# Turning three tiles by 32-column blocks by way of DRAM, with a clock for SyncE's queue in the planner

## The chip, the cores and the metric

The kernel runs on one core of one Trainium2 chip. The metric is the device time in microseconds of one execution. A profiled execution gives, beside its time, a trace of the instructions of each engine: PE (TensorE), DVE (VectorE), ACT (ScalarE), POOL (GpSimd) and SP (SyncE, which here only issues DMAs).

## The reference

One layer of a sequence mixer over 512 frames of 2048 channels. A combined projection feeds two groups of heads, RWKV-7 (16 heads of 64) and HGRN2 (8 heads of 128). Their gated outputs pass one output projection and a layer norm.

```python
proj = jnp.einsum('btd,dc->btc', h, w_in[l])
rw = _token_shift(proj[..., :RWKV_COLS], shift_mu[l])
hg = proj[..., RWKV_COLS:]
o_rwkv, v_first = _rwkv7_branch(rw, ...)
o_hgrn = _hgrn2_branch(hg, ...)
y = jnp.einsum('btc,cd->btd', jnp.concatenate([o_rwkv, o_hgrn], axis=-1), w_out[l])
h = _layer_norm(ALPHA * h + y, ln_w[l], ln_b[l])
...
# RWKV-7, per head, frame by frame, with a = -kk and b = kk * ah:
sa = jnp.einsum('bhij,bhj->bhi', S, a_t)
S = S * w_t[:, :, None, :] + sa[..., None] * b_t[:, :, None, :] + v_t[..., None] * k_t[:, :, None, :]
o_t = jnp.einsum('bhij,bhj->bhi', S, r_t)
```

## The kernel before

**The main stream.** The projections are made of tiles of 128 output channels by 512 frames, 16 steps of 128 input channels each. An fp32 product is made of three float32r matmuls (high by high, high by low, low by high), issued by `three` (line 453). Weights come in loads of 128x1024 into one of two buffers wr (`load`, line 430). Each half is split into a high part wh by ACT and a low part wl by DVE; there are three buffers of each, and `ready` asks for a part two parts ahead of its use. This stream of main matmuls is written out in order.

**The planner.** Everything else runs as Python generators that yield operations. A `Plan` keeps an estimated clock for each engine. After each main matmul it pumps its queues: it starts an operation on DVE, ACT or POOL when the operands are estimated to be ready, and it puts a small matmul between the main ones when its operands are due at least 0.35 us earlier (`LEAD`). What is decided is the order of each engine's instructions; on the chip semaphores hold an instruction until its operands are there. A DMA is issued on SP as the planner comes to it, and `plan.ready` gets an estimated landing time.

**The RWKV pairs.** Two heads make a pair, eight pairs in all, and two pairs make a group. `rwkv_prep` makes, per pair, tiles of 128 channels by 8 chunks of 64 frames: ar (from kk and r) and bk (beta and k). After the scores are made from them, bk is turned, so that the frames of a chunk stand on the partitions: `turned` (line 392) transposes the 32x32 blocks with DVE into a tile tmp and then moves each of the 4 x 4 blocks to its place with a DMA of its own (line 401), SBUF to SBUF, back into bk. The same is done with v into partitions 64 to 127 of a tile z ("zz"), with 4 x 2 blocks. Behind each four (or two) DMAs the generator waits for 0.4 us of PE's clock per DMA. Between the two turns stands the product that sums r k r_k over a head: ACT and DVE split r (tiles "ksq"), two matmuls with a block of ones follow, and the result times v is S["bv"].

**The scan.** `rwkv_group` inverts the scores of a group, adds what v alone gives (`from_v`, which writes partitions 0 to 63 of z), and then `rwkv_scan` goes through the 8 chunks: a product of the state with ar, one of the scores with rt, and one of bk with z that changes the state. `outputs` makes the group's outputs out of z, and `rwkv_finish` normalizes, gates and hands each pair on. `z[:, c]` in these functions is chunk c of z, 128 contiguous columns (2 heads x 64 channels).

Buffers of a pair: "q4" has six (ar, bk and tmp are three), "zz" two, "ksq" two.

Of the kernel before, what the change touches and what calls it, by code (L numbers as in the profile page):

```python
# [7 lines left out]
F32 = mybir.dt.float32  # L8
# [54 lines left out]
class Plan:  # L63
# [178 lines left out]
def mixer_kernel(ctx, tc, head, x_r, w_all, par, up, ln_wb, consts, hmask, out):  # L242
# [53 lines left out]
    def landed(*tiles):  # L296
# [9 lines left out]
        return test  # L306


    def size(ap):
# [81 lines left out]

    def turned(dst, src, tmp, rows=4, base=0):


        name = dst.tensor.name
        yield dtr(tmp, src)
        yield lambda: by_now(tmp)
        for a in range(4):
            for b in range(rows):
                o = base + 32 * b  # L400
                nc.sync.dma_start(dst[o : o + 32, :, 32 * a : 32 * a + 32],
                                  tmp[32 * a : 32 * a + 32, :, 32 * b : 32 * b + 32])
# [24 lines left out]
    def load(j):  # L427
        if j < nload:
            raws[j] = st("wr", [P, HALF])
            nc.sync.dma_start(raws[j], w_all[j - nhead])  # L430
            plan.fetched(raws[j], 4 * HALF)
# [116 lines left out]
    def constants():  # L548
        raw = st("ksq", [P, T])[:, : 16 * len(LEVELS)]
        for t, a in ((pr, par), (cst, consts), (raw, hmask)):  # L550
            nc.sync.dma_start(t, a)
# [48 lines left out]
    def put_gated(k, g):  # L600

        gated[k] = g
        if k in SPILL:
            def run():
                yield lambda: by_now(g)
                nc.sync.dma_start(spill[SPILL.index(k)], g)
                drop(g)

            plan.add(stores, run())
# [5 lines left out]
    def next_up():  # L615
        if len(ups) < NPAIR:
            upw = take("up", [P, 2, P])
            nc.sync.dma_start(upw, up[len(ups)])
            plan.fetched(upw, 8 * P)
            ups.append(upw)  # L620

    hc = [slice(64 * h, 64 * h + 64) for h in range(2)]

    def rwkv_prep(S, p):
# [114 lines left out]
        yield room(zz=1)  # L739
        z = take("zz", [P, NCH, P])  # L740
        yield room(ksq=1)
        tmp = take("ksq")
        yield from turned(z, chunks(v), chunks(tmp), rows=2, base=64)
        drop(v, tmp)
        S["zz"] = z

    def from_v(SS, sc):

        yield lambda: all("zz" in S for S in SS)
        zs = [S["zz"] for S in SS]  # L750
        yield room(main=2, mix=1)
        yield landed(*zs, sc)
        pss = [take("main") for _ in SS]
        for half, (z, ps) in enumerate(zip(zs, pss)):
            for c in range(NCH):
                for h in range(2):
                    yield mm(ps[hc[h], c * C : c * C + C], sc[64:128, 0, half * 16 + 2 * c + h],
                             z[64:128, c, hc[h]])

        def keep():  # L760
            for z, ps in zip(zs, pss):
                for h in range(2):
                    yield copy(z[0:64, :, hc[h]], chunks(ps[hc[h]]))
# [68 lines left out]
    def rwkv_scan(SS, sc):  # L832
# [9 lines left out]
        def block(ps, h):  # L842
            return ps[hc[h], h * 64 : h * 64 + 64]

        for rt, bds, o in zip(rts, bdss, os):
            yield memset(rt[64:128], 0.0)
            for t in bds:
                yield memset(t, 0.0)
            yield memset(o[0:64, 0], 0.0)
        olds = [None] * 2  # L850
        for c in range(NCH):
            more = c < NCH - 1
            zs = [zz[:, c] for zz in zzs]
            news = [bds[c % 2] for bds in bdss]
            pxs = []
            if c > 0:
# [5 lines left out]
                for rt, px, z in zip(rts, pxs, zs):  # L862
                    yield stt(rt[0:64], px[0:64, :P], -1.0, z[0:64], ALU.mult, ALU.subtract)
                if more:
                    for new, old, pc in zip(news, olds, pcs):
                        yield act(new, old, AF.Copy, scale=pc[:, c : c + 1])
            else:
                for rt, z in zip(rts, zs):
                    yield copy(rt[0:64], z[0:64], scale=-1.0)
            yield landed(*rts)  # L870
# [5 lines left out]
            for psa, z in zip(psas, zs):  # L876
                for h in range(2):
                    yield copy(z[0:64, hc[h]], block(psa, h))
                drop(psa)
# [17 lines left out]
    def rwkv_finish(S, p):  # L897
# [15 lines left out]
        yield has(S, "z", "bv")  # L913
        yield room(g=1, ksq=1)
        g = take("g")
        sz = take("ksq")
        z = S["z"]
        yield landed(o_all)
        po = take("mix")
        for j in range(4):  # L920
            yield tr(po[:, j * P : j * P + P], o_all[:, j])
        yield act(sz, z, AF.Tanh, scale=0.5)
        yield stt(g, po, hcol(HGW, p), S["bv"], ALU.mult, ALU.add)
        drop(po)
        yield stt(z, sz, 1.0, z, ALU.add, ALU.mult)
# [4 lines left out]
    def rwkv_group(SS, grp):  # L930
# [201 lines left out]
    scans = [plan.queue(), plan.queue()]  # L1132
    groups, finishes, preps = plan.queue(), plan.queue(), plan.queue()
    heads, stores = plan.queue(), plan.queue()
# [13 lines left out]
    def fetch(k):  # L1148
        raw = firsts[k] = take("q4", [P, T + FIRST * P])
        if k:  # L1150
            nc.sync.dma_start(raw, head[k])
        else:

            nc.scalar.dma_start(raw[:, T:], head[k, :, T:])
            for c in (slice(0, T // 2), slice(T // 2, T)):
                nc.sync.dma_start(raw[:, c], head[k, :, c])
        plan.fetched(raw, 4 * size(raw))
# [90 lines left out]
    def reload(n):  # L1248
        while len(asked) < min(n, KT):
            k = korder[len(asked)]  # L1250
            asked.append(k)
            if k in SPILL:
                plan.until(lambda: gated[k] is not None and (plan.free("t") or plan.free("g")))
                gated[k] = take("t" if plan.free("t") else "g")
                nc.sync.dma_start(gated[k], spill[SPILL.index(k)])
                plan.fetched(gated[k], 4 * T)
# [104 lines left out]
    def finish(t):  # L1361
# [4 lines left out]
        def norm():  # L1366
            ahead = []
            for d in range(5):
# [5 lines left out]
                if d:  # L1374
                    y, b, o, k = ahead.pop(0)
                    yield keyed(tt(y, y, b, ALU.add), k, k)
                    nc.sync.dma_start(o, y)

# [8 lines left out]
    def finish_last(t, pbs, weigh):  # L1387
# [16 lines left out]
        def norm():  # L1404
# [8 lines left out]
            for d in range(4):  # L1413
# [3 lines left out]
                for c in (slice(0, T),) if d < 3 else (slice(0, T // 2), slice(T // 2, T)):  # L1417
                    if d < 2:
                        yield keyed(stt(y, y, rs, b, ALU.mult, ALU.add), k + k_r, k)
                    else:  # L1420
# [3 lines left out]
                                    kc + k_r + [p.tensor.name], kc)  # L1424
                    nc.sync.dma_start(o[:, c], y[:, c])

# [26 lines left out]
    def residual(t, d):  # L1453
        plan.until(room(g=1))
        xrs[t] = take("g")
        nc.sync.dma_start(xrs[t], x_r[t, :, d * T : d * T + T])
        plan.fetched(xrs[t], 4 * T)
# [8 lines left out]
    def ahead(j, d):  # L1466

        if d == 0:
            split_gated(j + 2)
            if j == 8:  # L1470
                plan.until(room(big=1))
                lnw.append(take("big", [P, 2, D]))
                nc.sync.dma_start(lnw[0], ln_wb[None].to_broadcast([P, 2, D]))
                plan.fetched(lnw[0], 8 * D)
# [192 lines left out]
```

## Time and profile before

| | |
|---|---|
| time, median of 3 runs | 1050.54 us (1049.99 to 1050.96) |
| the profiled execution's own time | 1050.24 us |
| its span, first to last instruction | 1048.5 us |
| DMA | 114.79 MB in 87305 packets, 56368 of them under 512 B |
| mean granted TensorE clock | 0.999 |

The span is what the trace covers; 1.7 us of the profiled execution lie around it. A row of the page's groups reads: line, engine, operation, output and inputs, shapes, count, then the busy time and the mean ns of one, then the idle time of the engine ahead of them with what ended it. Matmuls overlap in the pipeline, so the mean ns of one is longer than the distance from one start to the next. A row of the waits reads: who waited, for whom, us in total, how often, and the longest.

### The profile page before, as it was taken

How to read it: one execution, taken by the hardware profiler on the slowest of the kernel's cores; microseconds unless marked ns; L12 is line 12 of the kernel's file. 1: busy time of each engine (PE TensorE's matmuls, PEld its weight loads, DVE VectorE, ACT ScalarE, POOL GpSimd, SP SyncE). 2: the span in 40 equal slices, each digit the busy share in tenths (PEclk: the TensorE clock that was granted, in tenths of full speed). 3: DMA queues.
4: the chain of work that ended last, by engine and by line, in shares of the span. 5: the costliest groups of instructions: out<-in, count | busy, mean ns of one | idle time of the engine just before them, and what ended most of it. 6: DMA issues, size and time to landing. Idle time of an engine off the chain costs nothing.

```text
span 1048.5 us, 18840 instructions
## 1 busy us (share of the span) xinstructions
PE 1040.6 (99%) x7342; PEld 865.1 (83%) x7342; DVE 755.7 (72%) x1653; ACT 437.6 (42%) x867; POOL 38.3 (4%) x81
## 2 busy tenths in 40 slices
PE   9999999999999999999999999999999999999997
PEld 8888888888888888888888888888888888888885
DVE  7465898667759987676689866865998778625556
ACT  6545333445353354452533353525334554323321
POOL 0000000000000000000000000000000002000000
PEclk9999999999999999999999999999999999999999
DMA  8134342222343522223534323234352244545613
GB/s 332 54 103 114 99 109 86 86 79 81 84 123 100 122 82 74 78 98 79 138 78 118 98 62 96 70 96 110 100 128 72 69 164 131 182 131 159 202 60 131
DMA packets 87305, 114.79 MB, mean 109 GB/s; under 512 B 56368, under 2 KB 58160, under 8 KB 87088
## 3 DMA queue, kind: packets, MB, share of 16 engines
q1 hardware_dynamic: 87072, 113.39, 36.6%
q8 instruction: 58, 0.95, 0.4%
q14 instruction: 31, 0.25, 0.1%
q10 hardware_dynamic: 144, 0.20, 0.1%
HBM read 99.92 MB, written 7.34 MB: 102 GB/s over the span
## 4 chain that ended last, share of the span: by engine, by line
PE 99%; DVE 1%; DVEq 0%; issue 0%
PE main L453 74%; PE mix L324 11%; PE mix L453 8%; PE main L1192 3%; PE main L324 2%; PE mix L328 1%; PE mix L1142 0%; DVE inv L356 0%; DVE inv L347 0%; DVE stats L1549 0%; DVEq L1663 0%; DVE mv L1357 0%; DVE bd L356 0%; DVE mv L352 0%; DVE inv L1140 0%
## 5 line engine op out<-in xcount | busy, mean ns | idle before, releaser
L453 PE MATMUL main<-xl,wh 128*128 128x512 f32 x864 | 341.1, 395 | 0.0
L453 PE MATMUL main<-xh,wl 128*128 128x512 f32 x864 | 341.1, 395 | 0.0
L453 PE MATMUL main<-xh,wh 128*128 128x512 f32 x864 | 340.9, 395 | 0.0
L337 ACT ACTIVATE wh<-wr 128x512 fp32r<-128x512 f32 x299 | 186.9, 627 | 237.1 <-PE main L453 180.5
L347 DVE TENSOR_TENSOR wl<-wr,wh 128x512 fp32r<-128x512 f32 x299 | 203.8, 682 | 61.8 <-ACT wh L337 60.1
L453 PEld LDWEIGHTS main<-xh,wh 128*128 128x128 f32 x864 | 162.4, 188 | 33.0
L453 PEld LDWEIGHTS main<-xh,wl 128*128 128x128 f32 x864 | 162.5, 188 | 32.6
L453 PEld LDWEIGHTS main<-xl,wh 128*128 128x128 f32 x864 | 162.4, 188 | 32.6
L453 PE MATMUL main<-wl,xh 128*128 128x512 f32 (+1 forms) x262 | 102.6, 392 | 0.0
L453 PE MATMUL main<-wh,xh 128*128 128x512 f32 (+1 forms) x262 | 102.1, 390 | 0.0
L453 PE MATMUL main<-wh,xl 128*128 128x512 f32 (+1 forms) x262 | 101.6, 388 | 0.0
L453 PEld LDWEIGHTS main<-wh,xh 128*128 128x128 f32 x262 | 49.2, 188 | 9.9
L453 PEld LDWEIGHTS main<-wh,xl 128*128 128x128 f32 x262 | 49.2, 188 | 9.7
L453 PEld LDWEIGHTS main<-wl,xh 128*128 128x128 f32 x262 | 49.2, 188 | 9.6
L338 ACT ACTIVATE t<-main,om 128x512 f32<-128x512 f32 x33 | 22.4, 687 | 51.1 <-PE main L453 41.6
L356 DVE SCALAR_TENSOR_TENSOR t<-main,pr,t 128x511 f32<-128x511 f32 x33 | 24.4, 747 | 26.5 <-ACT t L338 26.2
L347 DVE TENSOR_TENSOR inv<-inv,inv 64x30 f32<-64x30 f32 (+14 forms) x120 | 38.6, 322 | 2.9
L347 DVE TENSOR_TENSOR inv<-inv 64x30 f32<-64x30 f32 (+14 forms) x120 | 38.4, 320 | 2.3
L347 DVE TENSOR_TENSOR t<-t,tot 128x256 f32<-128x256 f32 x96 | 37.8, 414 | 1.8 <-PE mix L324 1.7
L356 DVE SCALAR_TENSOR_TENSOR bd<-mix,pc,bd 64x64 f32<-64x64 f32 x112 | 31.7, 283 | 7.5 <-PE mix L324 5.2
L337 ACT ACTIVATE zz<-mix 64x64 f32<-64x64 f32 x63 | 13.8, 220 | 46.9 <-PE mix L324 45.8
L338 ACT ACTIVATE t<-main 128x512 f32<-128x512 f32 x32 | 18.5, 598 | 30.7 <-PE main L453 30.2
(222 smaller groups left out, 1328.0 us busy)
## 6 DMA issues: line engine op xcount, KB each, us to landing
wr<-w_all SPq DMA_DIRECT2D x156, 512.0 KB, 3.6
q<-head SPq DMA_DIRECT2D x15, 448.0 KB, 5.9
q<-q SPq DMA_DIRECT2D x128, 32.0 KB, 2.4
g<-x_r SPq DMA_DIRECT2D x16, 256.0 KB, 3.8
spill<-g SPq DMA_DIRECT2D x12, 256.0 KB, 2.7
out<-q SPq DMA_DIRECT2D x12, 256.0 KB, 2.4
t<-spill SPq DMA_DIRECT2D x10, 256.0 KB, 4.2
zz<-ksq SPq DMA_DIRECT2D x64, 32.0 KB, 2.6
```

Of the source, the lines that this page charges most:

```text
L324: return Op([("pe", cost, lambda: pe.matmul(o, l, r, start=start, stop=stop, **kw))], [l, r], [o], mode="narrow" if narrow else "main" if ...
L328: return Op([("pe", 0.11, lambda: pe.transpose(o, i, ident))], [i], [o])
L337: return "act", cost, lambda: sc_e.activation(o, i, f, scale=scale)
L338: return "act", cost, lambda: sc_e.activation(o, i, f, scale=scale, bias=bias)
L347: return dve_op([a, b], o, lambda: dve.tensor_tensor(o, a, b, f), base=0.16 if o.shape[0] < P and size(o) == C and o.tensor.name in tags e ...
L356: return dve_op([a, b], o, lambda: dve.scalar_tensor_tensor(o, a, s, b, f1, f2), per=0.00113, base=0.085 if o.shape[0] == P else 0.25 if s ...
L453: pe.matmul(ps, l, r, start=first and i == 0, stop=last and i == 2)
L1192: pe.matmul(pss[a], *ops, start=k == 0 and low == of == 0, stop=k == KT - 1 and low == 1)
```

## The change

The two kinds of turns go by way of DRAM, in blocks of 32 columns, and the planner gets a clock for SP.

`send` issues every DMA of SP from now on and moves the new clock "sp" by 0.44 us. `fetched` counts a load's landing from that clock, with 1.8 in place of 2.0 us behind the transfer. `turned` makes one DMA that writes the whole transposed tile into a DRAM tile far, waits until 3.7 us behind it by the planner's clock, and then reads it back with one DMA for each 32 partitions of the result: for bk 1 + 4 DMAs in place of 16, for v 1 + 2 in place of 8. Each is sent only when the "sp" clock is not ahead of PE's. The destination is then due 3.5 us behind the last send.

What comes back has another order of columns: block a (of four) outermost, then the chunk, then 32 columns. For z this order is kept, and all readers and writers of z name it by `z[:, :, c]` and `z[:, hb[h]]`. For bk a copy puts the columns back in order, out of bk into tmp, and tmp takes bk's place as S["bk"].

There is also a second queue for `rwkv_finish`, so that the two pairs of a group can finish beside each other. The branch `p < 0` in `rwkv_finish` is never taken, since p runs from 0 to 7.

```diff
-        self.clock = {"pe": 0.0, "dve": 0.0, "act": 0.0, "pool": 0.0, "dma": 0.0}
+        self.clock = {"pe": 0.0, "dve": 0.0, "act": 0.0, "pool": 0.0, "sp": 0.0, "dma": 0.0}
...
-        self.clock["dma"] = max(self.clock["dma"], self.clock["pe"]) + size * 128 / 360e3
-        self.ready[tile.tensor.name] = (self.clock["dma"] + 2.0, "dma")
+        self.clock["dma"] = max(self.clock["dma"], self.clock["sp"]) + size * 128 / 360e3
+        self.ready[tile.tensor.name] = (self.clock["dma"] + 1.8, "dma")
...
+    def send(o, i):
+
+        nc.sync.dma_start(o, i)
+        plan.clock["sp"] = max(plan.clock["sp"], plan.clock["pe"]) + 0.44
...
-    def turned(dst, src, tmp, rows=4, base=0):
-        name = dst.tensor.name
-        yield dtr(tmp, src)
+    def turned(dst, src, tmp, base=0):
+        c = src.shape[1]
+        n = src.shape[2] // 32
+        yield dtr(tmp, src.rearrange("p c (b f) -> p b c f", f=32))
         yield lambda: by_now(tmp)
-        for a in range(4):
-            for b in range(rows):
-                o = base + 32 * b
-                nc.sync.dma_start(dst[o : o + 32, :, 32 * a : 32 * a + 32],
-                                  tmp[32 * a : 32 * a + 32, :, 32 * b : 32 * b + 32])
-            at = plan.clock["pe"] + 0.4 * rows
-            yield lambda: plan.clock["pe"] >= at
-        plan.ready[name] = (plan.clock["pe"] + 3.0, "dma")
+        far = dpool.tile([4, 32, n, c * 32], F32, tag=nm("far"), name=nm("far"))
+        yield lambda: plan.clock["sp"] <= plan.clock["pe"]
+        send(far.rearrange("a p b r -> (a p) b r"), tmp.rearrange("p b c f -> p b (c f)"))
+        at = plan.clock["sp"] + 3.7
+        plan.busy[tmp.tensor.name] = (at, "dma")
+        yield lambda: plan.clock["pe"] >= at
+        for b in range(n):
+            yield lambda: plan.clock["sp"] <= plan.clock["pe"]
+            o = base + 32 * b
+            send(dst[o : o + 32].rearrange("p a c f -> p a (c f)"), far[:, :, b].rearrange("a p r -> p a r"))
+        plan.ready[dst.tensor.name] = plan.busy[dst.tensor.name] = (plan.clock["sp"] + 3.5, "dma")
...
+    def blocks(t, c):
+
+        return t.rearrange("p (a c f) -> p a c f", c=c, f=32)
...
+    hb = [slice(2 * h, 2 * h + 2) for h in range(2)]
...
-        yield from turned(bk, bk, tmp)
-        drop(tmp)
+        flat = bk.rearrange("p c t -> p (c t)")
+        yield from turned(blocks(flat, NCH), bk, blocks(tmp.rearrange("p c t -> p (c t)"), NCH))
+        yield copy(tmp.rearrange("p c (a f) -> p a c f", f=32), blocks(flat, NCH))
+        drop(bk)
+        S["bk"] = tmp
...
-        z = take("zz", [P, NCH, P])
+        z = take("zz", [P, 4, NCH, 32])
...
-        yield from turned(z, chunks(v), chunks(tmp), rows=2, base=64)
+        yield from turned(z, chunks(v), blocks(tmp, NCH), base=64)
...
-                             z[64:128, c, hc[h]])
+                             z[64:128, hb[h], c])
...
-                                 sc[:, 1, half * 16 + 2 * (c + e) + h], z[:, c + e, hc[h]])
+                                 sc[:, 1, half * 16 + 2 * (c + e) + h], z[:, hb[h], c + e])
...
-            zs = [zz[:, c] for zz in zzs]
+            zs = [zz[:, :, c] for zz in zzs]
...
-                plan.add(finishes, rwkv_finish(S, 2 * grp + i))
+                plan.add(finishes[i], rwkv_finish(S, 2 * grp + i))
```

What stands in the queues now, at the places that the prediction speaks of. First SP, at the turns of the first pair, before (q_447 is bk, q_735 is tmp, ksq_833 the transposed v, wr the weight loads):

```order
L430 DMA wr_751<-w_all 128x1024
L401 DMA q_447<-q_735 32x8x32 x8
L430 DMA wr_794<-w_all 128x1024
L401 DMA q_447<-q_735 32x8x32 x8
L430 DMA wr_847<-w_all 128x1024
L401 DMA zz_832<-ksq_833 32x8x32 x8
L618 DMA up_894<-up 128x256
L430 DMA wr_917<-w_all 128x1024
```

And SP at the same place of the changed kernel, where far_762 and far_880 are the tiles in DRAM:

```order
L310 DMA wr_751<-w_all 128x1024
L310 DMA far_762<-q_735 128x1024
L310 DMA wr_788<-w_all 128x1024
L310 DMA q_447<-far_762 32x4x256 x4
L310 DMA wr_826<-w_all 128x1024
L310 DMA wr_876<-w_all 128x1024
L310 DMA far_880<-ksq_861 128x512
L310 DMA zz_860<-far_880 32x4x256 x2
L310 DMA up_918<-up 128x256
L310 DMA wr_942<-w_all 128x1024
```

24 DMAs have become 8, a weight load stands between the write to far and its reads, and the turn of v comes one weight load later than it did.

Next ACT at the same time, before (wh are the weight splits, ksq the split of r, t_858 a finished projection):

```order
L337 ACTIVATE wh_815<-wr_751 128x512
L337 ACTIVATE ksq_824<-t_460 128x512
L337 ACTIVATE wh_842<-wr_751 128x512
L338 ACTIVATE t_858<-main_755,om 128x512
L337 ACTIVATE wh_870<-wr_794 128x512
```

And ACT there in the changed kernel:

```order
L342 ACTIVATE wh_805<-wr_751 128x512
L342 ACTIVATE wh_821<-wr_751 128x512
L342 ACTIVATE q_735<-q_447 128x4x8x32
L342 ACTIVATE ksq_830<-t_460 128x512
L343 ACTIVATE t_839<-main_755,om 128x512
L342 ACTIVATE wh_848<-wr_788 128x512
```

The copy of bk into tmp is new in ACT's row, and the split of r has moved behind it and behind one more weight split. For seven of the eight pairs the copy stands on ACT, for one on DVE.

Last PE, behind the scores of the last pair, before (mix_7630 has the last scores, the transposes by cst belong to the finish of an earlier pair):

```order
L324 MATMUL mix_7629<-q_7459,q_7460 128x128
L324 MATMUL mix_7630<-q_7459,q_7460 128x128
L453 MATMUL main_7635<-xl_84,wh_7599 128x512
L453 MATMUL main_7635<-xh_68,wl_7600 128x512
L453 MATMUL main_7635<-xh_69,wh_7599 128x512
L453 MATMUL main_7635<-xl_85,wh_7599 128x512
L328 MATMUL mix_7662<-cst,t_5445 128x128 x4
L453 MATMUL main_7635<-xh_69,wl_7600 128x512
```

And PE there in the changed kernel:

```order
L329 MATMUL mix_7541<-q_7374,q_7375 128x128
L329 MATMUL mix_7542<-q_7374,q_7375 128x128
L333 MATMUL mix_7552<-cst,t_5278 128x128 x4
L470 MATMUL main_7544<-xl_85,wh_7507 128x512
L470 MATMUL main_7544<-xh_69,wl_7508 128x512
```

The four transposes now follow the scores at once, where four main matmuls stood between: two interruptions of the main stream have become one. Over the whole order there were 142 interruptions and there are 135; the matmuls are the same in number and shape.

More of the change, by code (lines that the diff above doesn't have):

```diff
@@ L429, in load @@
             raws[j] = st("wr", [P, HALF])
-            nc.sync.dma_start(raws[j], w_all[j - nhead])
+            send(raws[j], w_all[j - nhead])
             plan.fetched(raws[j], 4 * HALF)
@@ L550, in constants @@
         for t, a in ((pr, par), (cst, consts), (raw, hmask)):
-            nc.sync.dma_start(t, a)
+            send(t, a)
             plan.fetched(t, 4 * size(t))
@@ L605, in run @@
                 yield lambda: by_now(g)
-                nc.sync.dma_start(spill[SPILL.index(k)], g)
+                send(spill[SPILL.index(k)], g)
                 drop(g)
@@ L617, in next_up @@
             upw = take("up", [P, 2, P])
-            nc.sync.dma_start(upw, up[len(ups)])
+            send(upw, up[len(ups)])
             plan.fetched(upw, 8 * P)
@@ L762, in keep @@
                 for h in range(2):
-                    yield copy(z[0:64, :, hc[h]], chunks(ps[hc[h]]))
+                    yield copy(z[0:64, hb[h]], ps[hc[h]].rearrange("p (c a f) -> p a c f", c=NCH, f=32))
                 drop(ps)
@@ L868, in rwkv_scan @@
                 for rt, z in zip(rts, zs):
-                    yield copy(rt[0:64], z[0:64], scale=-1.0)
+                    yield copy(by32(rt[0:64]), z[0:64], scale=-1.0)
             yield landed(*rts)
@@ L877, in rwkv_scan @@
                 for h in range(2):
-                    yield copy(z[0:64, hc[h]], block(psa, h))
+                    yield copy(z[0:64, hb[h]], by32(block(psa, h)))
                 drop(psa)
@@ L913, in rwkv_finish @@
         yield has(S, "z", "bv")
-        yield room(g=1, ksq=1)
+        yield room(g=1)
         g = take("g")
+        if p < 0:
+            yield from turned(blocks(S["ot"], 4), o_all, blocks(g, 4))
+        yield room(ksq=1)
         sz = take("ksq")
         z = S["z"]
[L918 to L924, printed above, removed]
+        if p < 0:
+            yield act(in_blocks(g), blocks(S["ot"], 4).rearrange("p a c f -> p c a f"), AF.Identity,
+                      scale=hcol(HGW, p), bias=hcol(HGB, p))
+            yield act(sz, z, AF.Tanh, scale=0.5)
+            yield tt(g, g, S["bv"], ALU.add)
+        else:
+            yield landed(o_all)
+            po = take("mix")
+            for j in range(4):
+                yield tr(po[:, j * P : j * P + P], o_all[:, j])
+            yield act(sz, z, AF.Tanh, scale=0.5)
+            yield stt(g, po, hcol(HGW, p), S["bv"], ALU.mult, ALU.add)
+            drop(po)
         yield stt(z, sz, 1.0, z, ALU.add, ALU.mult)
@@ L1132, in mixer_kernel @@
     scans = [plan.queue(), plan.queue()]
-    groups, finishes, preps = plan.queue(), plan.queue(), plan.queue()
+    groups, finishes, preps = plan.queue(), [plan.queue(), plan.queue()], plan.queue()
     heads, stores = plan.queue(), plan.queue()
@@ L1150, in fetch @@
         if k:
-            nc.sync.dma_start(raw, head[k])
+            send(raw, head[k])
         else:
@@ L1155, in fetch @@
             for c in (slice(0, T // 2), slice(T // 2, T)):
-                nc.sync.dma_start(raw[:, c], head[k, :, c])
+                send(raw[:, c], head[k, :, c])
         plan.fetched(raw, 4 * size(raw))
@@ L1254, in reload @@
                 gated[k] = take("t" if plan.free("t") else "g")
-                nc.sync.dma_start(gated[k], spill[SPILL.index(k)])
+                send(gated[k], spill[SPILL.index(k)])
                 plan.fetched(gated[k], 4 * T)
@@ L1376, in norm @@
                     yield keyed(tt(y, y, b, ALU.add), k, k)
-                    nc.sync.dma_start(o, y)
+                    send(o, y)
         plan.add(norms, norm())
@@ L1424, in norm @@
                                     kc + k_r + [p.tensor.name], kc)
-                    nc.sync.dma_start(o[:, c], y[:, c])
+                    send(o[:, c], y[:, c])
         plan.add(norms, norm())
@@ L1455, in residual @@
         xrs[t] = take("g")
-        nc.sync.dma_start(xrs[t], x_r[t, :, d * T : d * T + T])
+        send(xrs[t], x_r[t, :, d * T : d * T + T])
         plan.fetched(xrs[t], 4 * T)
@@ L1472, in ahead @@
                 lnw.append(take("big", [P, 2, D]))
-                nc.sync.dma_start(lnw[0], ln_wb[None].to_broadcast([P, 2, D]))
+                send(lnw[0], ln_wb[None].to_broadcast([P, 2, D]))
                 plan.fetched(lnw[0], 8 * D)
```

6 lines of the change are left out of this document (5 added, 1 removed).

## The prediction

> **What bounds the kernel now.** I read the page first, then the waits of PE, then the waits of ACT and SP, and last the timeline of single stretches, since on a kernel with one full engine only a wait of that engine, or a change of its own work, can move the end.
>
> ```profile
> span 1048.5 us, 18840 instructions
> PE 1040.6 (99%) x7342; PEld 865.1 (83%) x7342; DVE 755.7 (72%) x1653; ACT 437.6 (42%) x867; POOL 38.3 (4%) x81
> ...
> PE 99%; DVE 1%; DVEq 0%; issue 0%
> ```
>
> The chain that ends last is PE for 99% of the span. The waits of PE in the whole execution are these three:
>
> ```profile
> PE mix L324 <- ACT ksq L1409: 1.5, 1, 1.5
> PE mix L1142 <- DVE inv L1140: 1.1, 1, 1.1
> PE mix L324 <- DVE bd L356: 0.4, 1, 0.4
> ```
>
> L1142 is the first instruction and L1409 the last step of the closing layer norm, so in all that the change touches PE waited 0.4 us. There is no wait here for the change to take away. It can pay only by making PE's own work cheaper, and it can cost by making PE wait.
>
> **What the change takes off SP.** Before, a turn is 16 DMAs for bk and 8 for the part of zz that comes from v.
>
> ```profile
> L401 SPq DMA_DIRECT2D q<-q x128: 585/608/1292, 74.9 to 768.5; - x128
> ...
> DMA to landing us min/median/max: 1.9/2.5/4.8
> ```
>
> ```profile
> 74.92 5.33 SPq L401 DMA_DIRECT2D q<-q  x8
> ...
> 80.94 5.16 SPq L401 DMA_DIRECT2D q<-q  x8
> ...
> 86.80 5.52 SPq L401 DMA_DIRECT2D zz<-ksq  x8
> ```
>
> ```profile
> SPq L430 <- DVE wl L347: 535.3, 106, 12.9
> ```
>
> One issue holds SP for 0.608 us, so 192 of them take 192 x 0.608 = 117 us of it. The new form has, for each of 8 pairs, 1 + 4 DMAs for bk and 1 + 2 for zz, 64 in all; at the same 0.608 us that is 39 us, so SP is relieved of about 78 us. What does that bring? SP's largest wait is 535 us for VectorE to be done with a weight buffer: SP stands idle for half of the span and sends a weight load as soon as its buffer is free. For the end, 78 us of SP's time are worth nothing unless a late load makes PE wait, and PE waits for none.
>
> **The turn's own length.** For the first pair the 16 bk issues go from 74.92 to 86.10 with a weight load between; the last begins at about 85.5, and with the median landing of 2.5 us the last piece is there 13 us after the first issue. Of the new route the trace shows no step, so each is bounded by its neighbours:
>
> ```profile
> wr<-w_all SPq DMA_DIRECT2D x156, 512.0 KB, 3.6
> ...
> spill<-g SPq DMA_DIRECT2D x12, 256.0 KB, 2.7
> ...
> up<-up SPq DMA_DIRECT2D x8, 128.0 KB, 3.2
> ```
>
> The write to far is 512 KB, to DRAM: between 2.7 us (half the size, same direction) and 3.6 us (same size, other direction); I take 3.6. The four reads are 128 KB each like the load of up: 3.2 us from issue to landing, and three issues ahead of the last at 0.608 us are 1.8 us. Together 3.6 + 1.8 + 3.2 = 8.6 us. The ends: 2.7 + 1.9 (the shortest landing of a small piece) + 1.8 = 6.4 us below, and above, where each hop stands behind a weight load as the slowest small piece did (4.8 instead of 1.9 us, so 2.9 more), 8.6 + 5.8 = 14.4 us. The planner's own due time for it is 0.44 + 3.7 + 4 x 0.44 + 3.5 = 9.4 us from the first send. So I expect the data about 0.8 us ahead of the due time, and the far end is 5 us behind it.
>
> **What is added on VectorE and ScalarE.** Each bk now needs a copy of 128x1024 (seven of the eight are on ACT, one on DVE, by the order), and the two transposes per pair read or write other strides.
>
> ```profile
> L366 DVE STREAM_TRANSPOSE q<-q 128x1024 f32<-128x1024 f32 x8 | 9.9, 1235 | 0.0
> ...
> L366 DVE STREAM_TRANSPOSE inv<-big 32x1024 f32<-32x1024 f32 x8 | 16.1, 2017 | 0.1
> ```
>
> ```profile
> L337 ACT ACTIVATE wh<-wr 128x512 fp32r<-128x512 f32 x299 | 186.9, 627 | 237.1 <-PE main L453 180.5 <-PE mix L453 32.9 <-DMA wr<-w_all 13.4
> ```
>
> A copy is at most two of 128x512, 2 x 0.627 = 1.25 us, so 10 us of ACT in all. A transpose stays at 1.24 us or becomes like the one that walks its input by another order, 2.02 us: 0 to 8 x 0.8 = 6 us for bk, and at the same ratio 0 to 3.5 us for v. I take zero, since the inner run of 32 stays contiguous. Both engines have room (ACT 42%, DVE 72%), and ACT spends 180.5 us waiting for PE to free a buffer before a wh split: it runs ahead of PE. The cover at the very place, the first bk, is seen in ACT's timeline:
>
> ```profile
> 82.33 0.63 ACT L337 ACTIVATE wh<-wr 128x512 fp32r<-128x512 f32 x1 [1.57 <-PE main L453]
> 85.80 0.69 ACT L338 ACTIVATE t<-main,om 128x512 f32<-128x512 f32 x1 [2.84 <-PE main L453]
> ```
>
> By the order the copy stands behind that split of 82.33; ACT then sits idle for 2.84 us. A far write issued where the first piece was, at 74.92, has its blocks back, by the 8.6 us above, at 83.5, and a copy of 1.25 us ends at 84.8, ahead of 85.80: it fits into that hole. If it did not, what follows is late; how much lateness PE stands is shown by another row:
>
> ```profile
> ACT wh L337 <- DMA wr<-w_all: 13.4, 5, 5.5
> ```
>
> ACT once stood 5.5 us before a weight split because a load had not landed, and none of PE's three waits is due to it. The weight path is covered; 0 us.
>
> **PE's own work.** The matmuls are the same in number and shape. Two things about them change.
>
> First, their places. Counted over the whole order, the stream of main matmuls is interrupted 142 times before and 135 times now. The price of one interruption:
>
> ```profile
> 191.47 0.40 PE L453 MATMUL main<-xh,wl 128*128 128x512 f32 x1
> 191.70 0.61 PE L324 MATMUL mix<-rt,big 128*128 128x128 f32 x4
> 192.06 0.48 PE L453 MATMUL main<-xh,wh 128*128 128x512 f32 x1
> 192.38 0.39 PE L453 MATMUL main<-xl,wh 128*128 128x512 f32 x1
> ...
> 193.31 0.49 PE L328 MATMUL mix<-cst,t 128*128 128x128 f32 x3
> 193.64 0.61 PE L324 MATMUL mix<-zz,q 128*128 128x128 f32 x4
> ```
>
> Start to start, a main matmul takes 191.70 - 191.47 = 0.23 us and a small pass (193.64 - 193.31) / 3 = 0.11 us. From the first small pass to the second main matmul behind it are 0.68 us; less 0.23 and 4 x 0.11 that leaves 0.01 us. For matmuls on part of the array the rows below leave more: main restarts at 188.37 and its row stands apart from the 64 passes ahead, which began at 187.69. I bound the price of an interruption by 0.01 and 0.3 us, seven of them by 0.1 and 2.1 us, and take 0.3 us in all, near the lower end, since whole-array interruptions are the ones that became fewer.
>
> Second, z is read as four runs of 32 columns, 1 KB apart, where it was 128 columns in a row. No row has this form; two others bound it.
>
> ```profile
> 157.17 0.70 PE L324 MATMUL mix<-t 128*32 128x16 f32 x62
> 157.74 0.70 PE L324 MATMUL mix<-t,t 128*32 128x16 f32 x62
> ...
> 174.03 0.70 PE L324 MATMUL mix<-t 128*32 128x16 f32 x62
> 174.59 0.70 PE L324 MATMUL mix<-t,t 128*32 128x16 f32 x62
> ...
> 180.91 2.08 PE L324 MATMUL main<-zz,big 64*64 64x64 f32 x64
> 182.92 1.11 PE L324 MATMUL mix<-inv,big 32*32 32x32 f32 x64
> ...
> 187.69 0.75 PE L324 MATMUL mix<-big,inv 32*32 32x32 f32 x64
> ```
>
> ```profile
> L324 PE MATMUL mix<-zz,q 128*128 128x128 f32 x112 | 17.2, 276 | 0.0
> L324 PE MATMUL mix<-zz,big 128*64 128x64 f32 x256 | 8.3, 224 | 0.0
> L324 PE MATMUL main<-zz,big 64*64 64x64 f32 x256 | 8.3, 220 | 0.0
> ```
>
> The HGRN scores move runs of 2 and 4 columns at 157.17 and runs of 8 and 16 at 174.03, and both take 0.57 us: runs cost nothing there. The other end is inv at 182.92, moved one column from each 128 bytes: 1.11 us against 0.75 us for the contiguous big, 48% more. On all z matmuls, 112 x 0.11 + 8.3 + 8.3 = 29 us, that would be 14 us. Runs of 32 are nearer to the first pair; I take 0.
>
> **The sum.** From the profiled execution, 1050.24 us with its span of 1048.5: interruptions -0.3, z reads 0, weights 0, and for a few short waits of PE where a step now comes at another time +0.5 (as much as the 0.4 us it had, once more). That is 1050.4; the median of the runs, 1050.54, lies 0.3 above the profiled one, so **1050.7 us**, no change that can be told: a measurement of this kernel tells about 0.2%, 2.1 us.
>
> **Rivals.** *ACT is held at the copy* (slower). Before, nothing on ACT waited for a turned bk; now seven copies do, and behind each in ACT's row stand the split of r for the sums of r k r_k (ksq<-t) and the next wh splits. PE's product of those sums follows at the planner's margin of 0.35 us, plus one main matmul, 0.23 us. The point of decision is data that land over 0.6 us behind the due time of 9.4 us, so after 10 us. At 1.5 us late each of the eight costs 0.9 us, 7 us in all: 1057; at the far end, 5 us late, 35 us. For it: the queue is shared with 512 KB loads and a small piece took up to 4.8 us. Against: 8.6 us and the hole of 2.84 us. Chance 0.13, most of it at 2 to 7 us. The Trainium skill, "DMA: Bandwidth & Descriptors", section "Anatomy of one DMA", puts most of a transfer's fixed 2 us on the receipt of the write and warns of a long delay when DRAM is the target, which speaks for this rival; by its fit, an estimate, the write would take 2.0 + 512 KB / 436 GB/s = 3.2 us and the last read 2.3 us, 7.3 us with the issues, and the forecast would stand; the trace's writes to DRAM, 2.7 us for 256 KB, agree with the fit's 2.6 us and show nothing of the warning.
>
> *The runs of z are slow*: 1050.7 + 14 = 1065. Chance 0.03; against it the equal 0.57 us.
>
> *The change does not free SP*: a read has to wait for the write's landing, and SP stands there with weight loads behind it. A wait of 3.6 us is inside the 5.5 us that PE did not feel, so the time stays, unless two fall together; 1053, chance 0.02.
>
> *Faster*: all seven interruptions at 0.3 us, and no new wait: 1050.54 - 2.1 = 1048.4. Chance 0.05. Nothing in PE's waits offers more.
>
> **How the numbers follow.** Forecast 0.77 (within 0.2% of 1050.54, that is 1048.4 to 1052.6), slower 0.13 + 0.03 + 0.02 = 0.18, faster 0.05. The range goes from 1048.9, where most of the interruptions' upper price is gained, to 1055, which takes in the nearer half of the held copy; the 14 us of the z reads and the far end of the copy stay outside with under 0.1.
>
> **What would show it.** PE's waits still under 3 us beside the first and last; no ACT wait at the copy's line for DMA over 1 us; issues of far and of the reads under 0.61 us each, landings near 3.6 and 3.2 us; mix<-zz,q still at 276 ns; the copy near 1.1 us. Wrong: a row of PE's waits with ksq or zz eight times, or zz,q matmuls over 300 ns, or a PE that is less than 99% busy.

## The result, and the profile after

The changed kernel takes 1056.78 us (median of 4 runs, 1056.17 to 1057.54) against 1050.53 us of the kernel before beside it. The ratio is 1.006, with an interval of 1.0045 to 1.0075: it is slower by 6.3 us, outside the range of 1048.9 to 1055.0. The profiled execution took 1056.37 us.

The page of the changed kernel, its span, busy engines and chain of work:

```profile
span 1054.6 us, 18711 instructions
...
PE 1043.0 (99%) x7342; PEld 867.1 (82%) x7342; DVE 751.2 (71%) x1636; ACT 449.1 (43%) x892; POOL 39.8 (4%) x81
...
PE 94%; DVE 2%; DMA 1%; ACT 1%; issue 1%; SPq 0%; POOL 0%; DVEq 0%; ACTq 0%
```

PE still counts as 99% busy; the loss of 6.1 us of span is 0.6%, too small for that figure. The chain shows it: PE fell from 99% to 94%, DVE has 2% in place of 1%, and ACT, a DMA and "issue" stand in it now. The waits of PE, and of ACT's the one for the blocks read back:

```profile
PE mix L329 <- ACT ksq L1442: 1.8, 1, 1.8
PE mix L329 <- issue: 1.8, 2, 1.3
PE mix L1175 <- DVE inv L1173: 1.1, 1, 1.1
PE mix L329 <- ACT zz L342: 1.0, 1, 1.0
PE mix L329 <- ACT ksq L342: 0.8, 1, 0.8
PE mix L329 <- DVE ksq L352: 0.5, 2, 0.2
...
ACT q L342 <- DMA q<-far: 16.3, 6, 3.5
```

Where 0.4 us of waits stood, four kinds are new. Each has a place in the timeline.

**The wait for "issue".** PE at 180 to 190 us (start, duration, engine, line, operation; idle time ahead and its releaser in brackets):

```profile
182.29 0.85 PE L329 MATMUL mix<-inv,big 32*32 32x32 f32 x43
184.47 0.52 PE L329 MATMUL mix<-inv,big 32*32 32x32 f32 x21 [1.33 <-issue]
184.92 0.60 PE L470 MATMUL main<-wh,xl 128*128 128x512 f32 x1
185.31 0.63 PE L470 MATMUL main<-xh,wh 128*128 128x512 f32 x1
...
188.30 0.53 PE L470 MATMUL main<-xl,wh 128*128 128x512 f32 x1
188.66 0.40 PE L470 MATMUL main<-xh,wl 128*128 128x512 f32 x1
```

PE stops 43 passes into a group of 64 like ones (the rows count passes, two to each of these small matmuls), with no semaphore to wait for. Behind the stop, nine main matmuls take 188.66 - 184.92 = 3.74 us, where nine at 0.227 us, the distance of the starts behind them, take 2.04: 1.7 us more. The same stretch by windows (stretch, its length, each engine's busy time, then the granted clock):

```profile
180.00:184.40 4.40, 3.14 (x143) 2.86 (x131) 2.00 (x6) 1.19 (x2) 0.00 (x0) 1.00 0.39 123
184.90:188.30 3.40, 3.40 (x13) 2.60 (x9) 2.25 (x7) 2.21 (x6) 0.00 (x0) 0.54 0.02 5
188.60:190.00 1.40, 1.40 (x7) 0.97 (x6) 1.39 (x6) 0.26 (x1) 0.00 (x0) 1.00 0.00 0
```

The granted clock fell to 0.54 for 3.4 us and then came back. PE counts as fully busy in that stretch, which is why the busy share hides it. The Trainium skill, "TensorE: Matmul & The Clock Gate", Part 1, lets the clock halve after an idle window of about 3.4 us and return after as long a busy one; the return agrees with these rows, but here a stop of 1.33 us was enough.

**The wait for ksq.** SP, ACT and PE of the changed kernel from 478 to 496 us:

```profile
479.53 0.42 SPq L310 DMA_DIRECT2D far<-q  x1
484.68 0.33 SPq L310 DMA_DIRECT2D q<-far  x1
...
486.53 0.86 SPq L310 DMA_DIRECT2D q<-far  x2
...
492.24 1.06 ACT L342 ACTIVATE q<-q 128x1024 f32<-128x1024 f32 x1 [3.50 <-DMA q<-far]
493.20 0.61 ACT L342 ACTIVATE ksq<-t 128x512 fp32r<-128x512 f32 x1
...
492.67 0.39 PE L470 MATMUL main<-xh,wl 128*128 128x512 f32 x1
493.86 0.49 PE L329 MATMUL mix<-ksq,ones_r 128*128 128x512 f32 x1 [0.81 <-ACT ksq L342]
494.59 0.50 PE L329 MATMUL mix<-ksq,ones_r 128*128 128x512 f32 x1 [0.23 <-DVE ksq L352]
```

ACT stands 3.50 us in front of the copy, the split of r stands behind the copy in its row, and PE stands in front of the product of that split. Here it cost 494.59 - 492.67 = 1.92 us less two starts of 0.23, so 1.46 us. At 333.6 us it cost 0.4 us in the same way, there by the part of the split that DVE makes behind ACT's.

**The wait for zz.** ACT at 444 to 451 us and PE at 450:

```profile
446.79 1.28 ACT L343 ACT_TABLE_LOAD   x1
...
449.80 0.43 ACT L342 ACTIVATE zz<-mix 64x64 f32<-64x64 f32 x2
...
450.29 0.38 PE L329 MATMUL mix<-zz,q 128*128 128x128 f32 x1 [1.00 <-ACT zz L342]
```

A step of the scan finds ACT occupied by the next pair's preparation, a table load and three operations of 128x512 behind it. This wait is an effect of the other order: it stands again in every run below that has this order of PE, and in none with another.

**The account.** Counted from start to start, so with the pipeline's refill behind an idle time: the stop 1.55 us, the half clock 1.7, the second "issue" wait (0.44 us idle at 825 us, in a group of 64 of t,t) 0.6, ksq 1.5 + 0.4, zz 1.2, the closing norm's wait 0.3 longer; less 0.55 us for the wait of before that is gone. That is 6.7 us. The last matmuls start 6.3 us later (1047.88 against 1041.55 us); the span grew by 6.1 and the median by 6.3. The 0.4 us that are left over are put to the fewer interruptions; they hold the errors of the other terms too.

### The profile page after: what moved, and what is told of

Same layout as the page of the kernel before. It is cut to its first block, busy times and chain, and to the rows that moved or that the text cites. A ratio compares the mean times of both kernels' runs of the same rounds, so it can differ in the third digit from the quotient of the medians.

```text
span 1054.6 us, 18711 instructions
## 1 busy us (share of the span) xinstructions
PE 1043.0 (99%) x7342; PEld 867.1 (82%) x7342; DVE 751.2 (71%) x1636; ACT 449.1 (43%) x892; POOL 39.8 (4%) x81
## 4 chain that ended last, share of the span: by engine, by line
PE 94%; DVE 2%; DMA 1%; ACT 1%; issue 1%; SPq 0%; POOL 0%; DVEq 0%; ACTq 0%
PE main L470 69%; PE mix L329 11%; PE mix L470 8%; PE main L1225 3%; PE main L329 2%; DMA q<-far 1%; PE mix L333 1%; DMA far<-q 0%; DVE wl L352 0%; PE mix L1175 0%; SPq L310 0%; ACT L343 0%; DVE inv L371 0%; DVE sm L365 0%; DVE ksq L352 0%
## 5 line engine op out<-in xcount | busy, mean ns | idle before, releaser
L342 ACT ACTIVATE zz<-mix 64x64 f32<-64x64 f32 x76 | 16.6, 219 | 31.2 <-PE mix L329 30.5
```

The source lines that it names most:

```text
L342: return "act", cost, lambda: sc_e.activation(o, i, f, scale=scale)
```

## The experiments

Theory A: the other order has put two groups of narrow matmuls (on part of the array) behind each other, and PE runs out of loaded instructions there. Theory B: PE stops there because the new transfers disturb something. Theory C: the blocks come later than the planner thinks, ACT stands in front of the copy, and PE is caught behind it.

What speaks for A: the queue of instructions, q8, moved 58 packets and 0.95 MB, 16 KB each, and 58 of them for 7342 matmuls and as many weight loads are 253 instructions each. By the order, the changed kernel has one run of 128 narrow matmuls behind each other (64 of t,t, 32 of zz,big and 32 of inv,big; in the trace each is two passes), and this is where PE stops. In the trace of the kernel before no run is over 64 (128 passes).

**The changed kernel again.**

> The changed kernel once more, for a second profile. Theory A (a run of 128 small matmuls on part of the array uses up PE's instructions faster than they come): the stop of about 1.3 us with releaser 'issue' inside mix<-inv,big near 183 us is there again, and eight or nine main matmuls behind it again take 0.43 us. Theory B (a chance delay of an instruction load behind other transfers): the stop is elsewhere or gone. Theory C (ACT is held at the copy of bk until the blocks land): waits of ACT for q<-far of about 16 us in all, and PE waits at ksq,ones_r of about 1.5 us in all, again.

1058.54 us, one run. The stop came back, 1.49 us with eight slow matmuls behind it, zz too, and ksq was 1.47 us:

```profile
PE mix L329 <- issue: 1.9, 2, 1.5
...
PE mix L329 <- ACT ksq L342: 1.5, 1, 1.5
```

Behind this longer wait for ksq, seven main matmuls took 0.427 us each; behind the 0.81 us of the first profile none did. So the waits belong to the order of the program, and the one that was some tenths longer cost 1.4 us more on top.

**No run over 64** (the changed kernel; the planner puts no further narrow matmul directly behind 64 of them).

```diff
         if op.mode == "narrow" != self.mode and now < self.rest:
             return False
+        if op.mode == "narrow" and self.mode != "main" and self.long >= 64:
+            return False
```

> The changed kernel with one more rule in the planner: no further matmul on part of the array directly behind 64 of them, so that the run of 128 becomes two of 64 with ten main matmuls between. The turns by DRAM stay. Theory A: the stop near 183 us and the slow matmuls behind it go, 1.5 + 1.8 = 3.3 us less, about 1053.5. Theory B (traffic delays the instruction loads): the stop stays, about 1056.8. Theory C alone: the order behind this place changes, but ACT still waits for q<-far about 16 us; PE waits at ksq,ones_r stay at 1 to 2 us.

1057.87 us, ratio 1.0061 (1.0048 to 1.0074). The total missed its expectation. The stop at 183 us is gone, but all that follows was planned anew, and the loss moved to C:

```profile
PE mix L332 <- ACT ksq L345: 3.7, 2, 2.2
...
PE mix L332 <- DVE ksq L355: 0.9, 2, 0.6
...
ACT q L345 <- DMA q<-far: 21.3, 6, 6.0
```

```profile
558.32 1.06 ACT L345 ACTIVATE q<-q 128x1024 f32<-128x1024 f32 x1 [6.04 <-DMA q<-far]
...
559.95 1.52 PE L332 MATMUL mix<-ksq,ones_r 128*128 128x512 f32 x2 [2.21 <-ACT ksq L345]
```

Not every long wait brings half clock. Behind the first of the two at ksq, the main matmuls of this kernel stand 0.23 us apart:

```profile
354.73 0.50 PE L332 MATMUL mix<-ksq,ones_r 128*128 128x512 f32 x1 [1.53 <-ACT ksq L345]
...
356.42 0.39 PE L473 MATMUL main<-xh,wl 128*128 128x512 f32 x1
356.65 0.40 PE L473 MATMUL main<-xh,wh 128*128 128x512 f32 x1
```

**Later due times** (the changed kernel, the write's 3.7 us set to 5.0 and the reads' 3.5 to 5.5).

```diff
-        at = plan.clock["sp"] + 3.7
+        at = plan.clock["sp"] + 5.0
...
-        plan.ready[dst.tensor.name] = plan.busy[dst.tensor.name] = (plan.clock["sp"] + 3.5, "dma")
+        plan.ready[dst.tensor.name] = plan.busy[dst.tensor.name] = (plan.clock["sp"] + 5.5, "dma")
```

> The changed kernel with later due times in the turns: 5.0 in place of 3.7 us behind the write to far and 5.5 in place of 3.5 us behind the last read. Theory C: ACT's wait for q<-far falls from 16 to under 4 us and PE's waits at ksq,ones_r go, 2 us less. Theory A: its order has a run of 128 small matmuls at another place, behind main matmul 2301 (about 600 us) and none at 735, so a stop with releaser 'issue' of over 1 us stands there with slow matmuls behind it, and none near 183 us. Both: about 1055. Theory B: no stop bound to that place.

1051.93 us, ratio 1.0012 (1.0003 to 1.0021). No wait of PE at ksq over 0.1 us is left, as C has it. But ACT's wait for the blocks was to fall under 4 us, and it did not; its longest is longer than the 3.5 us of the changed kernel:

```profile
ACT q L342 <- DMA q<-far: 12.8, 6, 4.4
```

A run of 128 is in this order too, at 605 us, but its stop is 0.18 us, not over 1: a run of that length is not enough for A.

**Both** (the cap and the later due times).

> Both edits, the cap at 64 and the later due times. Theories A and C together: no stop of PE without a releaser, no wait at ksq,ones_r, main matmuls at 0.43 us nowhere; 1056.8 - 3.3 - 2.0 = 1051.5, level with the kernel before within 1 us. If a third cause that belongs to the DRAM route stands behind the loss (z read in runs of 32, for one), it stays 2 us or more above the kernel before.

1050.48 us, ratio 1.0 (0.9992 to 1.0009).

**The planner's clock alone** (the kernel before with the clock "sp", `send`, the 1.8 us and the second finish queue; the turns stay inside SBUF).

> The planner's part of the change alone: the clock of SP, every DMA through send, the second queue for the finishes; the turns stay the 24 DMAs inside SBUF. If the loss comes with the turns by DRAM (theory C: ACT is held at the copy, which is not here), no wait of PE but the first and last and under 0.5 us between: 1050.5 within 1 us. If the planner's new clock itself makes a worse order (theory D), part of the 6 us is here: over 1052.5.

1051.3 us, ratio 1.0006 (0.9997 to 1.0014); no new wait of PE is over 0.3 us.

**The merged runs without the new turn** (the kernel before; the time that the planner leaves main matmuls ahead of a narrow group, 1.0 us, set to 5.0, so that groups collect. The order has runs of 128 behind main matmuls 733 and 1518, and two of 96).

```diff
-    HOLD = {"whole": 0.6, "narrow": 1.0}
+    HOLD = {"whole": 0.6, "narrow": 5.0}
```

> The kernel before, with small matmuls held for up to 5.0 in place of 1.0 us, which brings them together: its order has two runs of 128 on part of the array (behind main matmuls 733 and 1518) and two of 96; the turns stay inside SBUF. Theory A: inside at least one of the runs of 128 PE stops with releaser 'issue' for 0.2 to 1.5 us, how long by where the run meets the border of an instruction load, and where it is over 1 us main matmuls at 0.43 us follow. Theory B: with no transfers to DRAM in the turns no such stop, PE's waits with releaser 'issue' stay at nothing. The total may be 0 to 6 us above the kernel before, since other small work is late too.

1060.8 us, ratio 1.0099 (1.0084 to 1.0114). Its waits and its first stop:

```profile
PE mix L324 <- issue: 5.5, 4, 2.3
```

```profile
182.31 0.52 PE L324 MATMUL mix<-t,t 128*32 128x16 f32 x40
185.09 0.38 PE L324 MATMUL mix<-t,t 128*32 128x16 f32 x22 [2.26 <-issue]
```

Four stops: 2.26 and 1.76 us in the two runs of 128, 1.05 and 0.4 us in single groups of 64 of t,t; the two runs of 96 gave none. Behind the first two, seven main matmuls each ran at half speed; behind the one of 1.05 us none did. No tile of this kernel goes by way of DRAM for a turn, so B's transfers are not needed for it.

**The first or the second due time alone.**

> The changed kernel with only the wait between the write to far and its reads made longer, 5.0 in place of 3.7 us. The write's landing took 4.4 us at the median in the changed kernel. Theory C1 (it is the write that is late, and SP stands at the reads): ACT's wait for q<-far falls under 8 us and the time to about 1051.5. Theory C2 (the reads are late, they landed 4.1 us behind their issue at the median against 3.5): ACT's wait stays at 12 to 20 us, PE waits at ksq,ones_r of 1 us or more remain, 1053 to 1056.

> The changed kernel with only the due time behind the reads made later, 5.5 in place of 3.5 us. Theory C2: ACT's wait for q<-far falls under 10 us, PE waits at ksq,ones_r under 0.5 us, about 1051.5 to 1052. Theory C1: ACT's wait stays above 12 us and 1053 or more. Theory A: its order has a run of 128 small matmuls behind main matmul 2301 and none at 735: no stop near 183 us, one of 0.2 us or more near 600 us.

With 5.0 us behind the write alone: 1053.98 us, ratio 1.0032 (1.0021 to 1.0044); ACT still waits 20.1 us for the reads, and PE 1.2 + 0.2 us for ksq and 0.8 us for "issue", this one up to 413.63 us in a group of 64 of t,t. With 5.5 us behind the reads alone: 1050.38 us, ratio 1.0 (0.9991 to 1.0009). These are the waits of the second:

```profile
PE mix L329 <- ACT ksq L1442: 1.5, 1, 1.5
PE mix L1175 <- DVE inv L1173: 1.1, 1, 1.1
...
ACT q L342 <- DMA q<-far: 9.6, 4, 3.9
```

PE waits at its first and last steps only. So it is the reads' due time that is too early, not the write's. The later due time does not bring the blocks in time: ACT still waits 9.6 us, 3.9 us at the longest. What it moves is the product in PE's row. At that longest wait the copy starts at 716.64 and PE comes to the product at 719.61, 2.97 us behind, and at no pair is it less (2.73 us with both due times later). In the changed kernel it was 1.62 us at the wait of 0.81 us (492.24 and 493.86).

The run of 128 in this order, at 605 us, gave no stop at all, a miss of what was expected of A.

**The border moved** (the changed kernel with 16, or 32, more matmuls of 32x32 into the warm-up's tile at the start; the order behind them is the same, row by row. The added matmuls write nothing that is read.)

```diff
         pe.matmul(warm, zero, zero)
+    for _ in range(16):
+        pe.matmul(warm[:32, :32], zero[:32, :32], zero[:32, :32])
```

> The changed kernel with 16 more matmuls of 32x32x32 (64 lines of 16 or so instructions for the load of the code) into the warm-up's tile, right behind the warm-up; the order behind them is that of the changed kernel, row by row. Theory A (the stop at 183 us is the end of the loaded instructions inside a run of 128 short matmuls, so it depends on where the border of a load falls in the run): the stop of 1.33 to 1.49 us at 183 becomes another size or goes, and the half-speed matmuls behind it with it; total 1053 to 1058. Theory B (the matmuls there wait for data or for each other): the stop stays at 1.3 to 1.5 us, total 1056.5 to 1058. ACT's wait for the second turn of q is untouched: waits at ksq,ones_r at 333 and 492 us stay within some tenths.

> As the kernel with 16 more matmuls, but with 32. Theory A: a third size of the stop at 183 us, different from 1.33 to 1.49 us by over 0.3 in this kernel or in the one with 16; theory B: 1.3 to 1.5 us in both. Total 1053 to 1058 by A, 1056.5 to 1058 by B.

PE at the stop, with 16 more:

```profile
186.10 0.39 PE L329 MATMUL mix<-inv,big 32*32 32x32 f32 x11
188.31 1.00 PE L329 MATMUL mix<-inv,big 32*32 32x32 f32 x53 [1.82 <-issue]
```

And with 32 more:

```profile
182.39 1.49 PE L329 MATMUL main<-zz,big 64*64 64x64 f32 x43
186.09 1.43 PE L329 MATMUL main<-zz,big 64*64 64x64 f32 x21 [2.21 <-issue]
```

Sixteen matmuls are 32 passes, and the stop moved from behind pass 43 of inv,big to behind pass 11, 32 passes earlier; with 32 more it stands behind pass 43 of zz,big, another 32 earlier. In all three traces 1244 passes lie ahead of the stop. It keeps its distance from the start of the program, not its place in the computation: it is a border between two loads of instructions, and neither data nor an operand can be what PE waits for. The packets of q8 show the load (us, from the trace):

```
                    load begins   PE resumes   between
changed kernel         182.16       184.47       2.31
with 16 more           186.02       188.31       2.29
with 32 more           183.84       186.09       2.25
```

The totals are 1060.5 us, ratio 1.0085 (1.0063 to 1.0106), and 1059.42 us, ratio 1.0084 (1.0068 to 1.01), above what was expected of A: the stops are longer, the granted clock stays halved for 6.8 us where it was 3.4, and with 16 more thirteen main matmuls run at half speed behind the stop where it was nine, and eight more at the very start (7.0 to 10.6 us). The small second "issue" wait is gone in both.

**The copy behind the turn of v** (the changed kernel, due times as they were).

```diff
-        yield copy(tmp.rearrange("p c (a f) -> p a c f", f=32), blocks(flat, NCH))
-        drop(bk)
-        S["bk"] = tmp
         yield has(S, "v")
...
         drop(v, tmp)
+        yield copy(wide_bk.rearrange("p c (a f) -> p a c f", f=32), blocks(flat, NCH))
+        drop(bk)
+        S["bk"] = wide_bk
```

> The changed kernel with the same due times, but the copy of the beta-scaled k stands behind the turn of v in the list of steps, not ahead of it. Theory C (half of the loss is ACT standing in front of the copy, with the squares of the next pair behind it): ACT's wait for the reads of q falls from 16.3 us to under 4, no wait at ksq,ones_r is over 0.3 us, and the time is 1051 to 1054, the rest being stops within runs of short matmuls. Rival (the squares are late since ACT has more to do, wherever the copy stands): waits at ksq,ones_r of 0.8 us and more stay, total 1056 and over.

1051.19 us, ratio 1.0003 (0.9994 to 1.0013). ACT's wait for the reads is gone, and of PE's waits only one of 0.2 us is new:

```profile
PE mix L329 <- ACT ksq L1443: 1.5, 1, 1.5
PE mix L1176 <- DVE inv L1174: 1.1, 1, 1.1
PE mix L329 <- DVE t L352: 0.2, 1, 0.2
```

The copy costs ACT the same, only nothing that PE needs stands behind it. The longest run of this order is 88 and gave no stop, so this kernel shows C's half; that A's half went with it is luck of the new order.

## Why the prediction was wrong

**Right.** There was nothing to gain: SP was not what PE waited for, and the four variants with the turns by DRAM whose new waits of PE are 0.2 us at most, 1050.38, 1050.48, 1051.19 and 1051.93 us, stand within 0.2% of the time before, where the forecast was. SP's relief is real and worth nothing. These rows of the changed kernel answer the smaller terms: the issues, the copy and the reads of z.

```profile
L310 SPq DMA_DIRECT2D q<-far x32: 319/424/438, 79.8 to 769.9; - x32
...
L310 SPq DMA_DIRECT2D far<-q x8: 326/376/427, 74.7 to 764.9; - x8
```

```profile
L342 ACT ACTIVATE q<-q 128x1024 f32<-128x1024 f32 x7 | 7.4, 1061 | 16.3 <-DMA q<-far 16.3
```

```profile
L329 PE MATMUL mix<-zz,q 128*128 128x128 f32 x112 | 17.4, 276 | 1.0 <-ACT zz L342 1.0
```

An issue takes 0.38 to 0.42 us (bound 0.61), the copy 1.06 us (bound 1.25), and zz,q stays at 276 ns: runs of 32 columns cost nothing. The transposes of bk, taken as unchanged, are so: 1.23 us each, 1.24 before. Fewer interruptions gained some 0.4 us by the account (0.3 said).

**Wrong: the turn's own length, "3.6 + 1.8 + 3.2 = 8.6 us".** The landings are longer:

```profile
far<-q SPq DMA_DIRECT2D x8, 512.0 KB, 4.4
q<-far SPq DMA_DIRECT2D x32, 128.0 KB, 4.1
```

The first pair's copy starts 10.14 us behind its write (84.88 and 74.74), where 8.6 us to the data was said. At 479.53 us the first read goes out 5.15 us behind the write, the last of the four 2.3 us later, with a weight load and a spill between them, and the copy starts 12.7 us behind the write. For the seven copies on ACT that distance is 9.6 to 12.7 us; six of them made ACT wait. The point of decision, "data after 10 us", was named, and five of these six were past it. So the mechanism of the rival *ACT is held at the copy* happened. It was given 0.13, since the cover was checked at one place, the first pair. There the copy came 1.4 us later than the 83.5 us that were worked out, and PE did not feel it. Its price was off in a way that no mean shows: not 0.9 us at eight places but nothing at most of them, 1.5 and 0.4 us at two, and, in the second profile, 1.4 us of half clock on top of a longer one.

The sentence on the Trainium skill in that rival weighed "DMA: Bandwidth & Descriptors", section "Anatomy of one DMA": by its fit 7.3 us, by its warning of a long delay on writes to DRAM more. That fit is given for DMAs issued by GpSimd, and these are SP's. The measured 4.4 us for 512 KB are more than the 3.2 of the fit, but the reads, which write to SBUF, took 4.1 us against 2.3. So the excess is not one of writes to DRAM, and these rows do not show the warning.

**Wrong: "for a few short waits of PE ... +0.5".** This term took in all that another order does, and it held 3.85 us of stops and half clock (0.6 of it in a single group of 64) and 1.2 us at zz. The seven interruptions were counted as a gain, with both ends above nothing. But one way to have fewer interruptions is to put two narrow groups behind each other, and the merged group of 128 outran the load of its own instructions. The run stood in the order, though no stop of before, whose runs end at 64, shows a price for it. The page of the Trainium skill "Runtime: NRT & Kernel Launch", section "Instruction fetch mechanics", has the 16 KB blocks, as q8 shows them, and holds the crossing of a border to be mostly hidden; here it is hidden in the main stream and not always in narrow groups, 64 long or merged.

**Open.** Why a run of 128, of the same groups in another order, gave no stop or 0.18 us at 605 us in two kernels was not followed up; that the border fell elsewhere in the run would agree with the moved stop, but their loads were not shifted. So it also stays open whether the kernel before, with groups of 64, has no stop by its order or by where its borders fall: groups of 64 stopped by 0.44 us in the changed kernel, and by 0.4, 0.83 and 1.05 us in two others. Open too is what decides whether the half clock follows a wait. Behind 1.05 us and less none came. Behind 1.33 us and more within the stream it came every time but one, the 1.53 us at 354.73 us of the kernel with no run over 64.

## What to carry to other kernels

When a step gets a longer route, ask not whether its data come in time on the mean, but what stands behind its consumer in that engine's row, at every repetition: the remedy was to plan the reads 2 us later or to put the copy behind the work that PE needs, and with either one PE no longer waited for ksq. Later reads did it though ACT still stood up to 3.9 us, with PE's product at least 2.7 us behind the start of the copy. When a planner or scheduler decides the order, a changed estimate re-deals all of it; look through the new order for long runs of short matmuls before counting fewer interruptions as a gain. None of the variants beat the kernel before: on an engine that is 99% busy, relief of another one has nothing to give.

## What the hardware showed

A load of about 256 instructions took 2.25 to 2.31 us from its packet to PE going on, in the three kernels listed above, and a run of narrow matmuls can use up what is loaded faster than that: stops of 0.2 to 2.3 us, in the trace as waits for "issue". Behind stops and waits of 1.33 to 2.26 us within the stream the granted clock halved, with one exception at 1.53 us; 5 to 13 main matmuls then took 0.427 us in place of 0.227, which made 1.7 us in the changed kernel. In every trace here the changes of the granted clock stand whole multiples of 3.413 us apart; the halved stretches within the stream lasted 3.41 or 6.83 us.
